# The moving operand of the MLP's matmuls read from the last token to the first

## The chip, the cores and the metric

The kernel runs on one core of a Trainium2 chip. The metric is the time of one execution on the device in microseconds (us). The kernel before takes 845.86 us, the median of three runs (842.13 to 848.72 us).

## The reference

One layer of a hybrid decoder on 512 tokens of 1024 features: an attention branch and a recurrent branch, merged, and then an MLP. The change lies in the MLP alone, which is the last two lines:

```python
h = rmsnorm(x, norm_mix_g[l])
proj = jnp.einsum('bsd,de->bse', h, w_in[l])
...
x = x + jnp.einsum('bsd,de->bse', merged, w_out[l])
h2 = rmsnorm(x, norm_mlp_g[l])
up = jnp.square(jax.nn.relu(jnp.einsum('bsd,df->bsf', h2, w_up[l])))
x = x + jnp.einsum('bsf,fd->bsd', up, w_down[l])
```

Here `h2` is 512 x 1024, `w_up` 1024 x 4096 and `w_down` 4096 x 1024, all float32.

## The kernel before

**Layout.** Features lie on the 128 partitions and tokens along the free axis, so a matmul has a 128 x 128 block of weights as its stationary operand and tokens as its moving operand. The 512 tokens are two halves of 256. TensorE works in float32r; every operand is split into a rounded part (`hi`) and the rest (`lo`), and every product is three matmuls: weights hi by tokens hi, weights hi by tokens lo, weights lo by tokens hi (`for e, (l, r) in enumerate(((hi, 0), (hi, 1), (lo, 0)))`, lines 1387 and 1404). In the profile a weight tile is called `whi` or `wlo`.

**Stages.** The input projection, the attention and the recurrent branch take the first part of the execution, the merge and the output projection follow, and from line 1006 on the kernel does the MLP. Those earlier stages are not touched.

**The MLP by sums of blocks.** The MLP's two matrix products are cut into blocks of two by two: input features by output features by the two halves of tokens. Instead of eight products of blocks, seven are made, each of a sum of weight blocks with a sum of token blocks. They are named M1 to M7 and run in the order of `ORDER7`. The token blocks, and the sums and differences of them, are called forms:

- `h2` holds the eight forms of the MLP's input, `h2[:, r, i, f]`, with r the hi or lo part, i one of four groups of input features, and f the form; one form is 256 tokens of one half, and they lie next to each other in memory (4 bytes a token).
- `us` (the list `forms`) holds the seven forms of the squared activations for one chunk, `forms[n][:, r, f, h]`, again 256 tokens each.

**The work on TensorE.** `steps` lists every product: for four rounds d, the up products of two chunks of hidden features (kinds `up` and `uq`), then the down products (`dn`) of these. The first chunk of all (`pl`, plain) is done without sums: its matmuls take the two halves together, 512 columns. `product_go` issues a product of M1 to M7: 24 matmuls of 256 columns, from four groups of input, two blocks of output and the three hi/lo pairs. `plain_go` issues a plain one. All of them are written to PSUM banks called `acc`.

**After each product.** `up_posts` and `plain_posts` take a bank, add or subtract it elementwise to what the other products gave, apply relu and square and store a quarter; `form_tasks` and `totals` make the next forms from quarters, on ScalarE (ACT) for hi and VectorE (DVE) for lo. `down_posts` adds a bank to `x2`, the residual, which holds 512 tokens in their order, and for the last round scales it by the norm (`r2`) and stores it to `out`. Weights come by DMA from SyncE's queue (SP), some sums of weights by DMAs that accumulate from GpSimd's queue (POOL), and ACT and DVE split them into hi and lo.

**What sets the order.** Each piece of work is a `Task` with an engine and a duration that the program assumes (2.73 us for a product of 24 matmuls; DVE, ACT and load times by formula). A planner lays the tasks out by due times, tries 400 variations with a fixed seed, and issues them in the order of the best one. These durations are constants in the program; the access pattern of a matmul does not enter them.

Of the kernel before, what the change touches and what calls it, by code (L numbers as in the profile page):

```python
# [21 lines left out]
P = 128  # L22
# [17 lines left out]
def tile_block(ctx: ExitStack, tc: tile.TileContext, x, w_in, w_rga, w_rgx, w_pa, w_pr, w_o,  # L40
# [38 lines left out]
    def psum(tag):  # L79
        return pp.tile([P, 512], F32, tag=tag, name=tag, bufs=nb[tag])  # L80
# [230 lines left out]
    with tc.tile_pool(name="p1", bufs=1) as p1:  # L311
# [3 lines left out]
        I = InOrder(nc.tensor)  # L315
# [25 lines left out]
        for k0, k1 in pieces:  # L341
            u, kk = k0 // 4, slice(k0 % 4, (k1 - 1) % 4 + 1)
# [611 lines left out]
    h2 = fin.tile([P, 16 * 1024 + 64], F32R, name="h2")  # L954
    onesr = h2[:, :1]
    h2 = h2[:, 48:48 + 16 * 1024].rearrange("p (r i f s) -> p r i f s", r=2, i=4, f=8)
# [50 lines left out]
    ACT8 = {"M1": 0, "M4": 3, "M2": 2, "M5": 4, "M6": 5, "M7": 6, "M3": 7}  # L1007
# [44 lines left out]
    act = lambda columns: 0.1 + 0.00085 * columns  # L1052
    raw, units, quads, forms, banks = {}, {}, {}, [None] * 8, {}
# [250 lines left out]
    I = InOrder(nc.tensor)  # L1304
# [70 lines left out]
    def product_go(o, pairs, u, fresh):  # L1375
        kind, a, p = o
        b, f = (kind, a, BANK.get(p, "Y")), FORM[p]
        split_y = kind == "dn" and a[0] == 3 and b[2] == "Y"

        def go():  # L1380
            if fresh:
                banks[b] = (*banks.get(b, ()), psum("acc")) if split_y else psum("acc")
            hi, lo = units[o]
            for v in range(u.start, u.stop):
                d = banks[b][v][:, :256] if split_y else banks[b][:, 256 * v:256 * v + 256]
                for z, i in enumerate(pairs):
                    for e, (l, r) in enumerate(((hi, 0), (hi, 1), (lo, 0))):
                        act = h2[:, r, i, ACT8[p]] if kind != "dn" else forms[2 * a[0] + i // 2][:, r, f, i % 2]
                        I.matmul(d, l[:, i, P * v:P * v + P], act, start=fresh and z == e == 0 and (v == 0 or split_y),
                                 stop=i == 3 and e == 2, skip_group_check=True)  # L1390
        return go

    def plain_go(o, half):
        kind, a, p = o
        oc, kc = int(p[1]) % 2, int(p[1]) // 2

        def go():
            hi, lo = units[o]
            if kc == half == 0:
                for u in range(2):  # L1400
                    banks[kind, a, oc, u] = psum("acc")
            for m in range(4 * half, 4 * half + 4):
                u, i = (m // 4, m % 4) if kc else (m % 2, m // 2)
                for e, (l, r) in enumerate(((hi, 0), (hi, 1), (lo, 0))):
                    I.matmul(banks[kind, a, oc, u], l[:, i, P * u:P * u + P], h2[:, r, i, 2 * kc:2 * kc + 2], start=kc == i == e == 0, stop=kc == 1 and i == 3 and e == 2)
        return go

    for kind, a, p, pairs in steps:
        o = kind, a, p
        if kind == "pl":  # L1410
            oc, kc = int(p[1]) % 2, int(p[1]) // 2
# [190 lines left out]
```

## Time and profile before

| | us |
|---|---|
| median of three runs | 845.86 |
| lowest and highest run | 842.13, 848.72 |
| the profiled execution | 841.17 |
| its span, first to last instruction | 839.3 |
| the MLP's first matmul, from the span's start | 524.26 |

The mean granted clock of TensorE in the profiled execution is 0.999 of full speed. DMA moves 126.08 MB, on average 150 GB/s.

How to read the lines of the profile: a page has the busy time of each engine (PE is TensorE's matmuls, PEld its weight loads, DVE VectorE, ACT ScalarE, POOL GpSimd), a chain of work followed back from the last instruction, and groups of instructions. A group's line gives source line, engine, operation, output and input tile, shape and count, then after the bar busy time in us and the mean of one in ns, then the idle time before it and what ended it. L69 is the line of a helper that records the order of instructions; nearly everything in the MLP goes through it, so its groups are told apart by tile. Matmuls are pipelined: the mean duration of one is longer than the distance between two starts. A row of the timeline begins with the start and the duration in us; a row of the windows gives, for a stretch from one time to another, its length and then each engine's busy time and count, the granted clock, the share of DMA and GB/s.

### The profile page before, as it was taken

Reading aid. Unit: us, or ns where it says so; the run is one execution under the profiler, and the core shown is the slowest. Engines: PE = TensorE matmul, PEld = TensorE weight load, DVE = VectorE, ACT = ScalarE, POOL = GpSimd, SP = SyncE. Lnnn points to the kernel's source line nnn. Section 1 sums busy time; section 2 is a strip of 40 time slices with the busy share of each in tenths; the row PEclk is TensorE's granted clock in tenths of the full one; section 3 lists DMA queues with packets and bytes.
Section 4 is the critical chain, followed back from the end, with each engine's and each line's share of the span. In section 5 each row is a group of like instructions: output and inputs, shape, how many; then the busy total and the mean of one; then the engine's idle time right before and its main releaser. Section 6 shows DMA issues by size and latency. Waiting matters only on the chain.

```text
span 839.3 us, 14359 instructions
## 1 busy us (share of the span) xinstructions
PE 831.4 (99%) x5679; PEld 764.0 (91%) x5679; DVE 656.0 (78%) x1077; ACT 478.4 (57%) x753; POOL 104.2 (12%) x132
## 2 busy tenths in 40 slices
PE   9999999999999999999999999999999999999997
PEld 7899999999988888888888888899999999999997
DVE  6776688887877345978766767899889969977997
ACT  7445456565655334595663345784478358645932
POOL 0042231413201101111111000000000000000000
PEclk9999999999999999999999999999999999999999
DMA  5347232333322247656667672355565576566554
GB/s 202 122 151 222 89 107 71 103 115 97 88 79 76 88 138 209 197 171 187 178 199 165 207 258 74 101 151 152 178 174 146 158 256 171 141 166 198 151 160 117
DMA packets 41171, 126.08 MB, mean 150 GB/s; under 512 B 4992, under 2 KB 9800, under 8 KB 41104
## 3 DMA queue, kind: packets, MB, share of 16 engines
q1 hardware_dynamic: 31152, 92.65, 33.6%
q0 software_dynamic: 9952, 32.53, 17.7%
q8 instruction: 44, 0.72, 0.4%
q14 instruction: 23, 0.19, 0.1%
HBM read 102.05 MB, written 11.05 MB: 135 GB/s over the span
## 4 chain that ended last, share of the span: by engine, by line
PE 86%; DVE 8%; DMA 3%; issue 1%; ACT 1%; SPq 0%; ACTq 0%; DVEq 0%
PE acc L69 30%; PE acc L139 15%; PE acc L140 15%; PE acc L141 15%; DVE wlo L69 2%; PE at L595 2%; PE at L139 2%; PE at L141 2%; PE at L140 2%; DMA raw<-in_w_dn_dram 1%; PE at L631 1%; PE at L529 1%; DMA wraw<-in_w_in_dram 1%; DVE raw L69 1%; DVE x L69 1%
## 5 line engine op out<-in xcount | busy, mean ns | idle before, releaser
L69 ACT CAST whi<-raw 128x1024 fp32r<-128x1024 f32 x109 | 111.8, 1049 | 86.8 <-DVE raw L69 26.8
L69 PE MATMUL acc<-us,whi 128*128 128x256 f32 x896 | 153.6, 277 | 0.6 <-ACT us L69 0.4
L69 PE MATMUL acc<-h,whi 128*128 128x256 f32 (+1 forms) x848 | 153.2, 285 | 0.0
L69 DVE TENSOR_TENSOR wlo<-wraw,whi 128x1024 fp32r<-128x1024 f32 (+2 forms) x86 | 96.9, 1148 | 71.7 <-ACT whi L69 65.5
L69 DVE TENSOR_TENSOR wlo<-raw,whi 128x1024 fp32r<-128x1024 f32 x109 | 131.0, 1219 | 21.5 <-ACT whi L69 21.4
L69 PEld LDWEIGHTS acc<-us,whi 128*128 128x128 f32 x896 | 135.1, 188 | 1.1 <-ACT us L69 0.6
L69 PEld LDWEIGHTS acc<-h,whi 128*128 128x128 f32 x848 | 130.1, 188 | 2.6
L69 PE MATMUL acc<-us,wlo 128*128 128x256 f32 x448 | 124.0, 277 | 0.9 <-DVE wlo L69 0.9
L69 PE MATMUL acc<-h,wlo 128*128 128x256 f32 (+1 forms) x424 | 120.6, 285 | 0.0
L69 ACT CAST whi<-wraw 128x1024 fp32r<-128x1024 f32 (+2 forms) x86 | 82.5, 982 | 45.5 <-DMA wraw<-in_w_in_dram 30.4
L139 PE MATMUL acc<-whi,hT 128*128 128x256 f32 x384 | 108.4, 282 | 0.0
L140 PE MATMUL acc<-wlo,hT 128*128 128x256 f32 x384 | 107.2, 279 | 0.2 <-DVE wlo L69 0.2
L69 PEld LDWEIGHTS acc<-us,wlo 128*128 128x128 f32 x448 | 84.3, 188 | 1.1 <-DVE wlo L69 1.1
L139 PE MATMUL acc<-hT,whi 128*128 128x512 f32 x208 | 81.7, 393 | 0.0
L141 PE MATMUL acc<-hT,wlo 128*128 128x512 f32 x208 | 81.1, 390 | 0.0
L69 PEld LDWEIGHTS acc<-h,wlo 128*128 128x128 f32 x424 | 79.6, 188 | 1.3
L141 PE MATMUL acc<-whi,hT 128*128 128x256 f32 x288 | 80.2, 279 | 0.0
L69 ACT ACTIVATE pe<-pe,nm 128x128 f32<-128x128 f32 (+3 forms) x64 | 35.6, 558 | 66.2 <-DVE nm L69 66.2
L140 PEld LDWEIGHTS acc<-wlo,hT 128*128 128x128 f32 x384 | 72.5, 189 | 0.6 <-DVE wlo L69 0.4
L139 PEld LDWEIGHTS acc<-whi,hT 128*128 128x128 f32 x384 | 72.3, 188 | 0.5 <-issue 0.2
L69 POOL TENSOR_TENSOR rs<-ms,mhalf 128x8 f32<-128x8 f32 (+1 forms) x25 | 39.4, 1579 | 187.7 <-DVE ms L69 187.7
L69 POOL DMA_DIRECT2D raw<-raw x24 | 20.7, 864 | 325.0 <-DMA raw<-in_w_up_dram 89.4
(208 smaller groups left out, 1749.3 us busy)
## 6 DMA issues: line engine op xcount, KB each, us to landing
wraw<-in_w_in_dram SPq DMA_DIRECT2D x54, 512.0 KB, 3.6
raw<-in_w_dn_dram SPq DMA_DIRECT2D x32, 512.0 KB, 4.3
raw<-in_w_up_dram SPq DMA_DIRECT2D x29, 512.0 KB, 4.2
raw<-raw POOLq DMA_DIRECT2D x24, 512.0 KB, 4.6
sum<-in_w_up_dram POOLq DMA_DIRECT2D x18, 512.0 KB, 5.5
wraw<-in_w_pa_dram SPq DMA_DIRECT2D x8, 512.0 KB, 4.6
wraw<-in_w_pr_dram SPq DMA_DIRECT2D x8, 512.0 KB, 4.2
wraw<-in_w_o_dram SPq DMA_DIRECT2D x8, 512.0 KB, 5.1
```

What stands on the lines that cost most here:

```text
L69: ins = f(*a, **k)
L139: T.matmul(o, l[0], r[0], start=first, stop=False)
L140: T.matmul(o, l[0], r[1], start=False, stop=False)
L141: T.matmul(o, l[1], r[0], start=False, stop=last)
L529: T.transpose(out=ps[:, t * P:(t + 1) * P], in_=qn[t // 2][:, c0:c0 + P], identity=ident)
L595: T.matmul(lg[c][:, :N], qT[:, c, i * P:(i + 1) * P], qk[h % 2, z][:, c, :N], start=z == 1, stop=z == 2)
L631: T.transpose(out=tp[:, b * P:(b + 1) * P], in_=st[s][:, b * P:(b + 1) * P], identity=ident)
```

## The change

Three operands get a last index of `::-1`. In `product_go` the moving operand of the up products (a form of `h2`) and of the down products (a form of `us`) is read from token 255 of its half down to token 0. In `plain_go` the two halves stay in their order, and each is read backwards.

```diff
-                        act = h2[:, r, i, ACT8[p]] if kind != "dn" else forms[2 * a[0] + i // 2][:, r, f, i % 2]
+                        act = h2[:, r, i, ACT8[p], ::-1] if kind != "dn" else forms[2 * a[0] + i // 2][:, r, f, i % 2, ::-1]
                         I.matmul(d, l[:, i, P * v:P * v + P], act, start=fresh and z == e == 0 and (v == 0 or split_y),
                                  stop=i == 3 and e == 2, skip_group_check=True)
...
-                    I.matmul(banks[kind, a, oc, u], l[:, i, P * u:P * u + P], h2[:, r, i, 2 * kc:2 * kc + 2], start=kc == i == e == 0, stop=kc == 1 and i == 3 and e == 2)
+                    I.matmul(banks[kind, a, oc, u], l[:, i, P * u:P * u + P], h2[:, r, i, 2 * kc:2 * kc + 2, ::-1], start=kc == i == e == 0, stop=kc == 1 and i == 3 and e == 2)
```

A matmul writes its columns in the order in which it reads them, so every bank of the up products holds the tokens of a half in reverse, and so do the quarters and the forms made from it, since all that lies between is elementwise. The down products read those forms backwards once more, which puts the tokens into their old order in the banks that are added to `x2`. The weights, the addresses, the number of matmuls and the two matmuls of the norm (`norm_go`) are as before.

## Prediction

> **What bounds the kernel now.** I read the page's busy shares first, then its chain of work that ended last, then windows over the MLP, then the timeline of TensorE (PE) alone.
>
> ```profile
> span 839.3 us, 14359 instructions
> PE 831.4 (99%) x5679; PEld 764.0 (91%) x5679; DVE 656.0 (78%) x1077; ACT 478.4 (57%) x753; POOL 104.2 (12%) x132
> PEclk9999999999999999999999999999999999999999
> PE 86%; DVE 8%; DMA 3%; issue 1%; ACT 1%; SPq 0%; ACTq 0%; DVEq 0%
> ```
>
> TensorE is busy 99% of the span, the granted clock is in its top tenth in every slice, and 86% of the chain runs over TensorE. A change that alters how long one matmul holds the array therefore goes straight into the time. The next rows are the groups of the MLP (by line, shapes kept apart) and its start in the timeline.
>
> ```profile
> L69 PE MATMUL acc<-us,whi 128*128 128x256 f32 x896 | 153.6, 277 | 0.6 <-ACT us L69 0.4 <-DVE x L69 0.2
> L69 PE MATMUL acc<-h,whi 128*128 128x256 f32 x784 | 133.5, 276 | 0.0
> L69 PE MATMUL acc<-us,wlo 128*128 128x256 f32 x448 | 124.0, 277 | 0.9 <-DVE wlo L69 0.9
> L69 PE MATMUL acc<-h,wlo 128*128 128x256 f32 x392 | 108.2, 276 | 0.0
> L69 PE MATMUL acc<-h,whi 128*128 128x512 f32 x64 | 19.7, 389 | 0.0
> L69 PE MATMUL acc<-h,wlo 128*128 128x512 f32 x32 | 12.5, 389 | 0.0
> 524.26 0.62 PE L69 MATMUL acc<-h,whi 128*128 128x512 f32 x2
> ```
>
> The MLP runs from 524.26 us to the end. It has 896 + 784 + 448 + 392 = 2520 matmuls of 256 columns and 64 + 32 = 96 of 512; these are exactly the ones the change touches. TensorE's waits in these groups add up to 0.6 + 0.9 = 1.5 us, so the stage is bound by the matmuls themselves. The means of 276 and 277 ns are not what one matmul costs: they overlap. The cost is the distance from one start to the next. Stretches without a wait give it:
>
> ```profile
> core 0: us, PE busy (x) PEld busy (x) DVE busy (x) ACT busy (x) POOL busy (x), PEclk, DMA share, GB/s
> 571.60:628.90 57.30, 57.30 (x506) 57.30 (x507) 52.04 (x58) 30.33 (x37) 3.45 (x4) 1.00 0.63 177
> 660.50:792.80 132.30, 132.30 (x1170) 132.30 (x1169) 110.78 (x123) 84.43 (x108) 8.50 (x10) 1.00 0.62 176
> 821.20:834.90 13.70, 13.70 (x117) 13.70 (x118) 11.30 (x19) 2.17 (x3) 0.86 (x1) 1.00 0.41 109
> ```
>
> 132.30 us over 1170 matmuls is 113.1 ns each, and 57.30 over 506 is 113.2 ns. The last stretch is different: 13.70 over 117 is 117.1 ns, at the same granted clock of 1.00. So the same instruction on the same kind of operands has two paces. The timeline of TensorE around a short wait shows the change from one to the other:
>
> ```profile
> 642.59 0.28 PE L69 MATMUL acc<-us,wlo 128*128 128x256 f32 x1
> ...
> 647.69 0.28 PE L69 MATMUL acc<-us,wlo 128*128 128x256 f32 x1
> 648.14 0.47 PE L69 MATMUL acc<-us,whi 128*128 128x256 f32 x2 [0.17 <-DVE x L69]
> 648.45 0.28 PE L69 MATMUL acc<-us,wlo 128*128 128x256 f32 x1
> 648.80 0.28 PE L69 MATMUL acc<-us,wlo 128*128 128x256 f32 x1
> 649.15 0.28 PE L69 MATMUL acc<-us,wlo 128*128 128x256 f32 x1
> 649.51 0.28 PE L69 MATMUL acc<-us,wlo 128*128 128x256 f32 x1
> ```
>
> Products come in triples, so two wlo starts are three matmuls apart. From 642.59 to 647.69 there are 15 triples: 5.10 us / 45 = 113.3 ns. After the wait of 0.17 us, 648.45 to 649.51 are three triples: 1.06 us / 9 = 117.8 ns. The slower pace is therefore a state that a wait can start and that can last; I call the difference, 117.8 - 113.3 = 4.5 ns, the step. It is the only change of pace that the trace shows for these matmuls, and the trace doesn't say what makes it. A weight load runs beside every matmul (PEld is as busy as PE in the windows), so two reads of SBUF, one of the weights and one of the moving tokens, go on at all times; a pace that depends on how these two meet is what I would suspect.
>
> **The change part by part.** Nothing is added, removed or moved: the same 2616 matmuls with the same 2616 weight loads, outputs, waits and order, and no transfer, queue or other engine is touched. The planner's durations for a product are constants, so the order that it writes is the same one. What differs is the direction in which the moving operand is read.
>
> Step 1, the products of 256 columns. They read their half from token 255 down to 0. The cost is 2520 times the change of the pace, whatever that is; all of it lies on the path that sets the end. The trace of before has no operand that is read backwards, so the price is bounded from rows. The lower end is a gain of one step, 4.5 ns (if the backward order met the weight read better): 2520 x 4.5 = -11.3 us. The upper end of an ordinary loss is one step the other way, for those matmuls that do not have it yet. The last stretch has 117 at the slow pace and the one after 648.14 about a dozen: 2520 - 130 = 2390 x 4.5 = +10.8 us. A rougher bound from an earlier stage is the group below, whose mean is 282 ns beside 276 here: 6 ns, or 2520 x 6 = +15.1 us.
>
> ```profile
> L139 PE MATMUL acc<-whi,hT 128*128 128x256 f32 x384 | 108.4, 282 | 0.0
> 524.72 0.39 PE L69 MATMUL acc<-h,wlo 128*128 128x512 f32 x1
> 525.40 0.39 PE L69 MATMUL acc<-h,wlo 128*128 128x512 f32 x1
> 1.19 3.80 PE L69 MATMUL acc<-zero 128*128 128x256 f32 x17 [1.19 <-DVE zero L69]
> ```
>
> The far end is a read that delivers columns at half the rate. Its nearest row is the last one above, the slowest run of 256-column matmuls in the trace: 17 in 3.80 us, 224 ns each (an upper value, as the last one's drain is in it). That is 224 - 113 = 111 ns more, or 2520 x 111 = +279.7 us.
>
> Between these ends I take 0. The reason is a row pair: 512 columns in one matmul cost (525.40 - 524.72) / 3 = 227 ns, twice the 113.3 ns of 256 columns. The price is per column, with no part per instruction that shows, so it is the streaming that is paid for; a backward order asks for the same columns at the same distance of one element from each other. That value is nearest to the forward rows, which are the only ones of these very operands.
>
> [...]
>
> Step 2, the 96 plain products of 512 columns. Their operand becomes two runs of 256, each backwards, where it was one run of 512. Taken as two matmuls of 256 it costs 2 x 113.3 = 226.6 ns beside 227 measured: 96 x 0 = 0 us. One step more per half, 9 ns, would be +0.9 us; one less -0.9; half rate would be 96 x 2 x 111 = +21.3 us.
>
> Step 3, what follows. The banks now hold tokens in reverse within a half. The evacuations, squares, sums and splits are elementwise and see the same shapes: 0 us. The down products read the reversed forms backwards again, so their banks, the final scaling and the stores are as before: 0 us. The cover here is that no instruction of DVE, ACT or a queue changes; if it failed, any of them would be longer and TensorE would wait on DVE, which is busy 52.04 of 57.30 us (91%) in the densest stretch and is what comes late next.
>
> The sum is 0 + 0 + 0. Against the profiled execution's own time of 841.17 us (839.3 us of span and 1.9 us around it) this is 841.2 us. That execution stands 4.7 us below the median of the runs, 845.86 us (842.13 to 848.72). I give the time on the median's scale: **845 us**, rounded.
>
> **The rivals.**
>
> First, the slower one: the slow pace everywhere. Place: all 2616 matmuls. Mechanism: reading from the other end turns round the phase between the moving stream and the weight stream, and the state that now follows a wait becomes the usual one. Price: +10.8 + 0.9 = +11.7 us, or 852.9 us for the profiled execution and 857.6 us on the median's scale. It decides (over 1%, 8.5 us) from 8.5 / 2520 = 3.4 ns per matmul, which is less than the step. For it speaks that the two paces exist for one instruction; against it, that 1170 matmuls in a row over many different tiles hold 113.1 ns, so the fast state is not delicate. [...]
>
> Second, half rate: the array's read cannot stream downwards at full rate. Price: +279.7 + 21.3 = +301 us, 1147 us on the median's scale. For it speaks only that no row shows a backward read; against it, that the step stays one element.
>
> Third, faster: the backward order takes the step away from the usual pace. Price: -11.3 - 0.9 = -12.2 us, 833.7 us on the median's scale, if DVE keeps up; its 91% in the densest stretch would become 52.04 / (57.30 x 108.8 / 113.3) = 95%, so a little of it would come back as waits. [...] Against it: nothing in the trace shows any such matmul below 113 ns.
>
> Fourth, that the change doesn't do what it says: an access pattern could be turned into something else on the way to the chip. The counts would then differ (more matmuls of fewer columns); I hold it to be part of the second rival's chance.
>
> **How the numbers follow.** No change (within 1%) 0.55; slow pace or an ordinary loss of that size 0.17; half rate or another heavy loss 0.16; faster 0.12. About 1% is what a measurement of this kernel can tell from no change. So faster by over 1% is 0.12, within 1% 0.55, slower by over 1% 0.33. The range goes from the third rival, 834 us, up to the rough bound of an ordinary loss: 845.86 + 15.1 + 0.9 = 861.9, and some 3 us more for the runs' own spread (845.86 to 848.72), 865 us. It leaves out the heavy case, 0.16. The likeliest case's own range is 842 to 849 us, that of the runs before.
>
> **What would show each step right or wrong.** Right: start-to-start distances of 113 ns in the long stretches of the MLP and 227 ns for the 96 plain ones, counts of 896, 784, 448, 392, 64 and 32 unchanged, the MLP beginning near 524 us as before. The first rival shows as some 1170 matmuls in 138 us instead of 132.30 with PEclk still at 1.00, the second as a doubled distance and DVE's share falling to about half, the third as 109 ns and new waits of PE on DVE wlo. If the distances are unchanged and the span is not, the prediction is wrong outside its steps, in the waits or the transfers that this change should leave alone.

## The result, and the profile after

| | kernel before | changed kernel |
|---|---|---|
| median of 20 runs, us | 847.41 | 850.79 |
| lowest and highest | 840.68, 852.42 | 849.27, 856.96 |
| profiled execution | 841.17 | 851.39 |
| its span | 839.3 | 849.6 |

The changed kernel takes 1.007 times as long as the one before (95% interval 1.0047 to 1.0094): slower by some 0.7%, within the 1% that the prediction called no change, but clear of zero. The two profiled executions are farther apart, 10.2 us or 1.2%. Why the profiled executions differ by more than the medians is part of the finding.

The page of the changed kernel first: its span, the busy engines and the clock, and the chain of work that ended last.

```profile
span 849.6 us, 14359 instructions
PE 843.2 (99%) x5679; PEld 775.0 (91%) x5679; DVE 656.1 (77%) x1077; ACT 479.9 (56%) x753; POOL 103.7 (12%) x132
PEclk9999999999999999999999999999999999999999
PE 88%; DVE 5%; ACT 3%; DMA 2%; issue 1%; SPq 0%; ACTq 0%; DVEq 0%
```

TensorE's busy time rose by 11.8 us (831.4 to 843.2) with the same count of instructions. DVE and ACT are as busy as before (656.0 and 656.1, 478.4 and 479.9 us) and the granted clock is the same (0.999 and 1.000). So the time went into the matmuls themselves. The windows of the changed kernel, over the same stretches as before, show how:

```profile
571.60:628.90 57.30, 57.30 (x487) 57.14 (x486) 50.47 (x56) 28.01 (x34) 3.00 (x4) 1.00 0.61 175
660.50:792.80 132.30, 132.30 (x1126) 132.30 (x1125) 106.50 (x119) 77.85 (x98) 8.60 (x10) 1.00 0.61 171
```

In the same 132.30 us there are 1126 matmuls where there were 1170. A window also counts a matmul that only overlaps its edge, and a matmul overlaps one or two others (276 ns long at 113 ns from start to start in the kernel before), so the count is about 2.5 too high. Taking that off, 132.30 / 1123.5 = 117.8 ns, where the kernel before has 132.30 / 1167.5 = 113.3 ns. From here on paces are worked out in this way. The plain products changed, too, as the groups and the timeline of the changed kernel show:

```profile
L69 PE MATMUL acc<-h,whi 128*128 128x512 f32 x64 | 20.6, 401 | 0.2 <-DVE h L69 0.2
524.88 0.40 PE L69 MATMUL acc<-h,wlo 128*128 128x512 f32 x1
525.58 0.40 PE L69 MATMUL acc<-h,wlo 128*128 128x512 f32 x1
```

Their mean is 401 ns where it was 389, and the distance is (525.58 - 524.88) / 3 = 233 ns where it was 227. The 0.2 us at the end of the first row is TensorE's only listed wait in the MLP, where the kernel before had 1.5 us.

The sum of the two profiles: 2390 matmuls x 4.5 ns = +10.8 us (the prediction's count of those that had the fast pace), 96 x 6.5 ns = +0.6 us (the means of the distances are 233.3 and 226.8 ns), waits 0.2 - 1.5 = -1.3 us, together +10.1 us. The spans differ by 849.6 - 839.3 = 10.3 us. Nothing of size is left over.

### The profile page after: what moved, and what is told of

It reads as the page before. It is cut to its first block, busy times and chain, and to the rows that moved or that the text cites. A ratio compares the mean times of both kernels' runs of the same rounds, so it can differ in the third digit from the quotient of the medians.

```text
span 849.6 us, 14359 instructions
## 1 busy us (share of the span) xinstructions
PE 843.2 (99%) x5679; PEld 775.0 (91%) x5679; DVE 656.1 (77%) x1077; ACT 479.9 (56%) x753; POOL 103.7 (12%) x132
## 4 chain that ended last, share of the span: by engine, by line
PE 88%; DVE 5%; ACT 3%; DMA 2%; issue 1%; SPq 0%; ACTq 0%; DVEq 0%
PE acc L69 37%; PE acc L139 14%; PE acc L140 14%; PE acc L141 13%; PE at L595 2%; PE at L139 2%; PE at L140 2%; PE at L141 2%; DVE wlo L69 2%; DMA wraw<-in_w_o_dram 1%; PE at L631 1%; ACT whi L69 1%; PE at L529 1%; PE at L668 1%; DMA xT<-in_x_dram 1%
## 5 line engine op out<-in xcount | busy, mean ns | idle before, releaser
L69 PE MATMUL acc<-h,whi 128*128 128x256 f32 (+1 forms) x848 | 159.2, 291 | 0.2 <-DVE h L69 0.2
L69 PE MATMUL acc<-us,whi 128*128 128x256 f32 x896 | 158.7, 282 | 0.0
```

What stands on the lines that cost most here:

```text
L69: ins = f(*a, **k)
```

## The experiments

The theory at the start was that the pace hangs on how the moving read and the weight read meet in SBUF ("phase", later "meeting"). That was the author's guess, from two paces of one instruction (113.3 and 117.8 ns) with a weight load beside every matmul (1169 beside 1170 in 132.30 us); no run here shows such a meeting. By it, moving the weights should undo what turning the read round had done, and of blocks of tokens their order alone should count. Its rival was that a backward read costs by itself ("direction"). In the tables below, a pace is 100 us over the count less 2.5, from the window of 680 to 780 us, in which none of these kernels has a wait of TensorE. A time is one run, unless a range stands with it; the kernel before ran beside it.

### Weights moved by 64 or 128 bytes, in both directions

```diff
-            units[o] = weight_pair((0 if own else 64) if o[0] != "pl" else 192 if own else 0, fin if own else None)
+            units[o] = weight_pair((((0 if own else 64) if o[0] != "pl" else 192 if own else 0) + 64) % 256, fin if own else None)
```

This is put on the changed kernel (`rev_w64`) and on the kernel before (`fwd_w64`); `rev_w128` and `fwd_w128` add 128 in place of 64. The sum is taken modulo 256, so a tile that lay at 192 goes to 0 or 64.

> The changed kernel, with every weight tile of the MLP moved by 64 bytes. [...] Direction theory (a backward read costs 4 ns per 256 columns wherever it starts): 117 ns and about 850 us, as in the changed kernel.

> The kernel before, reading forward, with every weight tile of the MLP moved by 64 bytes. [...] Direction theory: 113.3 ns and about 840 us.

> The changed kernel, with every weight tile of the MLP moved by 128 bytes. Meeting theory with a period of 128 bytes: as the changed kernel, 117.8 ns. With a period of 256 bytes or more: another pace, between 113 and 121 ns. Direction theory: 117.8 ns.

> The kernel before, with every weight tile of the MLP moved by 128 bytes. Meeting theory with a period of 128 bytes: 113.3 ns, as in the kernel before, since 64 bytes gave 118.7 ns and another 64 close the period. With a longer period: another pace, 116 to 121 ns. Direction theory: 113.3 ns.

The window's rows, in the order rev_w64, fwd_w64, rev_w128, fwd_w128:

```profile
680.00:780.00 100.00, 100.00 (x836) 100.00 (x835) 77.89 (x86) 57.69 (x72) 5.16 (x6) 1.00 0.62 180
```
```profile
680.00:780.00 100.00, 100.00 (x845) 100.00 (x845) 78.90 (x87) 57.87 (x73) 5.16 (x6) 1.00 0.62 179
```
```profile
680.00:780.00 100.00, 100.00 (x836) 100.00 (x835) 77.58 (x85) 57.44 (x72) 5.16 (x6) 1.00 0.62 179
```
```profile
680.00:780.00 100.00, 100.00 (x851) 100.00 (x851) 79.14 (x87) 58.43 (x75) 5.16 (x6) 1.00 0.62 182
```

| kernel | pace, ns | time, us | kernel before, us |
|---|---|---|---|
| rev_w64 | 120.0 | 855.87 | 849.15 |
| fwd_w64 | 118.7 | 852.22 | 849.15 |
| rev_w128 | 120.0 | 857.65 | 850.48 |
| fwd_w128 | 117.9 | 851.33 | 850.48 |

The two runs with 64 bytes go against both theories. Moving the weights did not bring the backward read to 113.3 ns, it made it slower (120.0 beside 117.8); and the forward read lost its 113.3 ns without being turned round (118.7). The runs with 128 bytes go against the direction theory and against a period of 128 bytes; they lie in the ranges that a longer period left, but these held nearly every pace there is here. One window of a forward stream is weak evidence, as the repeats of the kernel before will show: 117.9 ns occurs with the weights in their old place, too. The address of the weights still mattered to a forward stream. That is seen at the very start of the MLP, before any wait: the forward plain products had a mean of 389 ns in the kernel before, and have it in all six profiles here that read them forward with whole blocks of weights in their old place (before, before_a, before_b, fwd_kick, fwd_wide, dn_back). They have 395 in fwd_w64, in the row below, and in fwd_w128.

```profile
L69 PE MATMUL acc<-h,whi 128*128 128x512 f32 x64 | 20.1, 395 | 0.0
```

So where the weights lay changed the mean of matmuls whose moving operand had not been touched, from 389 to 395 ns. What makes the difference, the rows don't show.

### Blocks of 16 tokens: only the order of the blocks, or only the order within a block

```diff
+                        act = act.rearrange("p (g c) -> p g c", c=16)[:, ::-1, :]
```

This is `lines_back`, put on the forward operand; `inline_back` has `[:, :, ::-1]` instead. The plain products get the same within each half.

> Each half is read in blocks of 16 tokens (64 bytes): the blocks from last to first, the 16 tokens in a block forward. [...] Direction theory, if what costs is the step of -1 from token to token: 113.3 ns. If blocks cost something by themselves: more than 117 ns.

> Each half is read in blocks of 16 tokens (64 bytes): the blocks from first to last, the 16 tokens in a block backward. [...] Direction theory, if what costs is the step of -1 from token to token: 117 ns.

Rows of the window, lines_back and then inline_back:

```profile
680.00:780.00 100.00, 100.00 (x851) 100.00 (x850) 78.47 (x88) 58.52 (x74) 5.64 (x7) 1.00 0.61 179
```
```profile
680.00:780.00 100.00, 100.00 (x752) 100.00 (x752) 74.98 (x82) 53.05 (x66) 6.88 (x8) 1.00 0.53 141
```

lines_back ran at 100 / 848.5 = 117.9 ns (850.72 us), the changed kernel's pace, and from its first products to the end, although its tokens go forward within every 64 bytes. So a step of -1 from token to token is not needed for that pace; turning round the order of the blocks is enough. This is one profile, without disturbances, and a forward stream can be at 117.8 ns as well. But the single distances, which the section on one kind of product explains, are those of a backward stream here. The reverse mixture was a surprise: inline_back ran at 100 / 749.5 = 133.4 ns (891.91 us), slower than anything else here and than either theory had it (113.3 ns by the phase theory, 117 by the direction theory). Why a jump after every 16 tokens added nothing to the changed kernel's pace in one kernel (117.9 ns) and 15.5 ns in the other (133.4) is open.

### Weights read from one column

```diff
-                        I.matmul(d, l[:, i, P * v:P * v + P], act, start=fresh and z == e == 0 and (v == 0 or split_y),
+                        I.matmul(d, l[:, i, P * v:P * v + 1].broadcast_to([P, P]), act, start=fresh and z == e == 0 and (v == 0 or split_y),
```

The matmul of `plain_go` gets the same. This is put on the kernel before (`fwd_onecol`) and on the changed kernel (`rev_onecol`). If the pace hangs on how the two reads meet, both directions should then have one pace.

> [...] Direction theory: 113.3 ns here.

> The changed kernel (backward), with every weight load of the MLP reading one column 128 times, as in the run before it. Meeting theory: the same pace as in that run, within 0.5 ns. Direction theory: some 4 ns slower than that run (117 to 118 ns).

Rows of the window, fwd_onecol and then rev_onecol; behind each a row of the same kernel from the first up products (TensorE alone: length, busy time and count, clock, DMA):

```profile
680.00:780.00 100.00, 100.00 (x860) 100.00 (x859) 79.58 (x88) 61.20 (x78) 6.03 (x7) 1.00 0.61 177
```
```profile
551.00:565.00 14.00, 14.00 (x126) 1.00 0.57 175
```
```profile
680.00:780.00 100.00, 100.00 (x852) 100.00 (x851) 78.49 (x88) 59.52 (x76) 6.03 (x7) 1.00 0.59 176
```
```profile
551.00:565.00 14.00, 14.00 (x121) 1.00 0.54 157
```

Forward it ran at 116.6 ns and backward at 117.7 ns (847.95 and 849.98 us), so the meeting theory fell: with the weight read standing still, the directions should have been alike within 0.5 ns. But the plain direction theory doesn't hold either, as 116.6 is not 113.3. The second row gave the next idea. In 551 to 565 us, its first up products, the same forward kernel ran at 14.00 / 123.5 = 113.4 ns, where the backward one has 14.00 / 118.5 = 118.1; it has 116.6 ns only after the one listed wait of TensorE in its MLP (0.4 us, on ACT). One kernel, one direction, two steady paces. So a new theory: the pace is a pattern that the stream of matmuls falls into when it starts or is interrupted, and then keeps.

### The kernel before, twice more

> The kernel before, unchanged, once more. Its runs lie in two groups, about 841 to 843 and 846 to 852 us. Locked-pace theory (the pace of the matmuls is a steady pattern that is set when the stream starts or is interrupted, and forward reading has both a 113.3 ns pattern and slower ones): a run of the upper group shows the MLP's matmuls at 116 to 120 ns for most of the MLP, with no more waits than before. Other theory (the groups come from waits on transfers): 113.3 ns in both groups and 5 to 9 us more of waits in the upper one.

> As the run before it: a second draw of the kernel before, with the same two expectations.

Two stretches of before_a, and the same two of before_b:

```profile
575.00:630.00 55.00, 55.00 (x469) 55.00 (x469) 48.20 (x53) 28.91 (x36) 3.44 (x4) 1.00 0.57 167
670.00:720.00 50.00, 50.00 (x443) 50.00 (x442) 41.17 (x46) 32.85 (x44) 2.84 (x4) 1.00 0.69 196
```
```profile
575.00:630.00 55.00, 55.00 (x488) 55.00 (x487) 49.71 (x55) 30.95 (x39) 3.44 (x4) 1.00 0.60 168
670.00:720.00 50.00, 50.00 (x427) 50.00 (x426) 39.81 (x44) 33.19 (x44) 2.58 (x3) 1.00 0.66 194
```

before_a (842.68 us) ran 55.00 / 466.5 = 117.9 ns in the first stretch and 50.00 / 440.5 = 113.5 in the second; before_b (845.81 us) the other way round, 113.3 and then 117.8. It is the same program, at the same clock. The forward stream has two patterns, and a short wait can move it from one to the other: before 648.14 us the kernel before has 113 or 114 ns from start to start, and behind the wait of 0.17 us there 117 to 119. It need not: all three profiles of this kernel have the same wait of 0.4 us on ACT near 570 us, and only before_a runs at 117.8 ns behind it. Nor need the wait be long: before_b changes between 647 and 649 us, where TensorE has no listed wait, only two places where the starts fall behind by some 0.15 and 0.26 us. From the MLP's first matmul to its last, the profiled executions of 841.17, 842.68 and 845.81 us take 311.0, 312.6 and 316.3 us, so nearly all that sets them apart lies in the MLP. The runs of the kernel before are spread over 840.68 to 852.42 us, eight of twenty below 844 and the others above 845. That the slowest of them have 117.8 ns nearly throughout fits this, but none of the runs above 846 us is profiled here, so it is not shown. The execution that the prediction worked from was one of the former, with nearly all its MLP at 113.3 ns. The changed kernel has no run below 849.27.

### Some forty short disturbances, forward and backward

```diff
+                        if fresh and z == e == 0 and v == u.start:
+                            n = 16 * (1 + 5 * len(kicks) % 16)
+                            kicks.append(n)
+                            I.matmul(d[:, :n], l[:, i, P * v:P * v + P], act[:, :n], start=True, stop=False, skip_group_check=True)
```

Here `kicks` is a list that starts empty. What the extra matmul writes is written over by the next one.

> The kernel before, with a short extra matmul ahead of the first one into each fresh bank of the MLP (16 to 256 columns, another width each time; what it writes is written over), which shifts the stream's phase about a hundred times. Locked-pace theory: the pace changes from product to product, and some of them run at 113.3 ns, others at 116 to 120 ns. Direction theory: 113.3 ns throughout, whatever the shift.

> The changed kernel with the same extra matmuls. If the backward read has the 113.3 ns pattern too and merely started in a slower one: some products at 113.3 ns, about as many as in the forward run. If the backward read doesn't have that pattern: no product below about 116.5 ns, though the pace changes from product to product.

Four stretches between disturbances of fwd_kick, then three of rev_kick (length, TensorE's busy time and count, clock, DMA):

```profile
571.50:585.50 14.00, 14.00 (x126) 1.00 0.62 179
588.90:594.20 5.30, 5.30 (x47) 1.00 0.39 74
595.20:608.20 13.00, 13.00 (x117) 1.00 0.59 213
608.60:613.80 5.20, 5.20 (x47) 1.00 0.84 293
```
```profile
572.40:587.40 15.00, 15.00 (x130) 1.00 0.63 176
597.00:607.50 10.50, 10.50 (x92) 1.00 0.57 201
637.20:648.00 10.80, 10.80 (x92) 1.00 0.62 177
```

Forward: 113.4, 119, 113.5, 117 ns; the stream goes to and fro between two paces, 113.3 and 117.8 (the short stretches are rough). Backward: 117.6, 117.3, 120.7 ns. Over the whole of rev_kick the stretches lie at 117.5 to 118.1 or at 120.0 ns; none is near 113.3. This is the run that decides: a backward stream was disturbed 47 times (not the hundred that the expectation named), by widths from 16 to 256 columns, and never fell into the 113.3 ns pattern that the forward one reached again and again. The times are 851.97 and 858.08 us, beside 843.71 for the kernel before.

### One kind of product backward

```diff
+                        act = act[:, ::-1] if kind == "dn" else act
```

This is `dn_back`, on the forward operand; `up_back` is the changed kernel without the `::-1` on the down products.

> Only the down products (1344 matmuls) read backward; the forms they read are not reversed, so the two halves of what the MLP adds come out with their tokens reversed. If the direction of a matmul alone sets its pace: 117.8 ns in the down products, 113.3 ns in the up products after them. If a pattern, once slow, is carried on by the matmuls that follow: 117.8 ns in the up products from the second round on as well, until a wait happens to set the fast pattern.

> Only the plain and up products (96 and 1176 matmuls) read backward, and the result's tokens are reversed within each half for the MLP's part. If the direction alone sets the pace: about 117.8 ns in the up products, 113.3 ns in the down products. If the pattern is carried on: the down products, reading forward, stay at 117.8 ns until a wait happens to set the fast pattern.

Stretches of dn_back: backward down products of the first round, forward up products of the second, forward up products of the third. Below them up_back: forward down products of the first round with backward up products of the second, then forward down products of the second, then backward up products of the third.

```profile
572.00:605.50 33.50, 33.50 (x287) 1.00 0.53 158
606.00:640.00 34.00, 34.00 (x303) 1.00 0.66 200
690.00:724.00 34.00, 34.00 (x291) 1.00 0.55 143
```
```profile
575.00:645.00 70.00, 70.00 (x597) 1.00 0.60 173
656.00:685.00 29.00, 29.00 (x258) 1.00 0.67 200
686.00:725.00 39.00, 39.00 (x333) 1.00 0.62 175
```

dn_back: 117.8, 113.1 and 117.9 ns. up_back: 117.7, 113.5 and 118.0 ns. The backward products are at 117.8 in every row. The forward ones can be at either: dn_back's were back at 113.3 ns in the second round and at 117.8 in the third, and up_back's at 117.7 in the first round and 113.5 in the second.

It looks as if the slow pattern were carried on into forward products sometimes. The single distances say otherwise. The trace holds starts to the nanosecond, and products come in triples. In a backward stretch of these two kernels, the three distances of a triple are 115, 118 and 120 ns (now and then 119 for 118), over and over. In a forward stretch at 117.8 ns, here and in before_a and before_b, they are 117 to 119 ns. Both add up to some 353 ns a triple, so the two have one mean and are still two patterns. In a forward stretch at 113.3 ns they are 113 or 114 ns.

At each of the fourteen places where these two kernels go over from one kind of product to the other, the distances change to those of the new direction within four matmuls, and there is no wait at any of them. Where forward turned to backward it was always 115, 118 and 120; where backward turned to forward it was 113.3 ns five times and 117 to 119 ns twice (dn_back at 684 us, up_back at 568 us). So in these two kernels the direction of the read set the pattern within four matmuls, and the backward pattern is not carried on. What chooses between the two forward ones is open. lines_back has the 115, 118 and 120 of a backward read throughout. The changed kernel has distances from 114 to 121 ns, with the same mean. rev_onecol is the exception: with the weights read from one column, its backward read has 117 to 119.

The times, 847.87 and 847.64 us, are single runs inside the range of the kernel before beside them (13 runs, 840.36 to 850.81 us), so they don't say what each half of the change costs.

### Putting the forward stream right on purpose

```diff
+                        if fresh and z == e == 0 and v == u.start and p == "M1":
+                            I.matmul(banks[b][v] if split_y else banks[b], l[:, i, P * v:P * v + P], h2[:, 0, 0, 0:2], start=True, stop=False, skip_group_check=True)
```

> The kernel before with one extra matmul of 512 columns ahead of the first product of every group of seven (some 15 of them, about 3.6 us; what they write is written over). [...] If that restores the fast pattern: every group starts at 113.3 ns, whatever the one before it ran at, a span of about 843 us and runs that lie closer together than those of the kernel before, which could be some 1 to 3 us below it in the median. If not: groups at 117.8 ns after a wait as before, and some 3 us more than the kernel before.

Four groups of seven products in a row, each begun by a wide matmul:

```profile
587.70:606.20 18.50, 18.50 (x165) 1.00 0.50 147
606.70:626.10 19.40, 19.40 (x167) 1.00 0.71 215
626.60:645.20 18.60, 18.60 (x167) 1.00 0.60 165
645.70:665.50 19.80, 19.80 (x169) 1.00 0.47 141
```

113.8, 117.9, 113.1, 118.9 ns: the wide matmul doesn't restore the pattern, it changes over from one to the other each time (with some 165 matmuls to a stretch these are rough by up to 1 ns; the single starts give 113.3 and 117.8 in turn). The expectation failed, and the kernel is slower than the one before: 851.22 us (849.1 to 853.16), ratio 1.0056 (1.0021 to 1.0091). No version here was shown to be faster than the kernel before.

## Why the prediction was wrong

**What bounds the kernel: right.** The MLP hangs on the distance between matmuls; all of the difference was found there.

**Step 1 failed.** It took a backward read of 256 columns for free, because the price looked like one per column and the distance from token to token stayed one element. The pair of rows behind this, 227 ns for 512 columns and 113.3 for 256, compares two forward streams, and cannot tell what a backward one costs. The change measured 4.5 ns on each of 2390 matmuls, +10.8 us between the profiles, the upper end of an ordinary loss that the step itself had named. What it lacked: the 113.3 ns were not the price of a column but one of two patterns of the forward stream, and the backward stream was never seen in it (rev_kick, and the fourteen changes of direction in dn_back and up_back). That the loss came out as one step, 4.5 ns, is luck: the step was read from the forward stream's own slow pattern, and the backward stream has another one with the same mean.

**Step 2** was 0 and measured 6.5 ns on 96 matmuls, +0.6 us. The comparison with two matmuls of 256 was nearly sound, but with those at 117.8 ns, not at 113.3: twice 117.8 is 235.6, and 233.3 was measured.

**Step 3: right.** DVE and ACT kept their busy time, and TensorE's waits fell from 1.5 to 0.2 us, likely because slower matmuls gave DVE more time (busy 50.47 of 57.30 us where it was 52.04; an estimate of the author's).

**The scale failed, too.** The prediction said that its execution stood 4.7 us below the median and moved its sum onto the median as it was. (0 on that scale is 845.86, which rounds to 846 and not to 845.) That gap was the finding in small: runs of the kernel before already have part of the MLP at 117.8 ns (before_a, before_b), so the change can take less from its median than from the profiled execution. 10.2 us between the profiles became 3.4 us between the medians.

**The first rival** had the pace right: 1126 matmuls in 132.30 us at clock 1.00, where it named 1170 in 138, and 852.9 us for the profiled execution where 851.39 was measured. Its time on the median's scale, 857.6, was too high for the reason just given. The argument held against it, that 1170 matmuls in a row at 113.1 ns show the pattern not to be delicate, was wrong: before_b loses it in the middle of the MLP, between 647 and 649 us, and has 117.8 ns in 670 to 720 us and in 740 to 790. The rival's mechanism is another matter. The state that follows a wait did not become the usual one, since the backward read has its own pattern (115, 118 and 120 ns); and the phase between the two reads is not shown: with the weight read on one column, the directions still differ (116.6 and 117.7 ns).

**The others fell.** Half rate: the cost is 4% (4.5 of 113.3 ns), not 100%. Faster: no 24 backward matmuls in a row are below 117.7 ns in the changed kernel, and no stretch of rev_kick is near 113.3. The change left out on the way to the chip: counts are unchanged and the pace is not.

The measured 850.79 us lies in the range, and within 1%, but the forecast was 845 and no change, and there was one. That the number is so near is luck: the loss that step 1 put at nothing shows in the median as a third of its size, because the kernel before is slow in many of its own runs.

## What to carry to other kernels

Before pricing a change to a stage that is bound by matmuls, look at the distance between starts over the whole stage, not at one mean: two steady values at one granted clock (here 113.3 and 117.8 ns at 1.00) show that the stream has patterns, and a change can cost the difference without touching any work (here 4.5 ns on each of 2390 matmuls). When the profiled execution does not stand at the median of its runs, ask what the others did before moving a sum from one to the other; two more profiles of the same kernel would have shown it. Keep the moving operand forward and contiguous where there is a choice: no other order tried here was seen at 113.3 ns (the windows of 100 us have 117.7 to 133.4). And a mean can hide a difference: two streams of 117.8 ns were told apart only by their single distances.

## What the runs showed that was not expected

The paces of 256-column matmuls are a handful of steady values, not a spread: 113.3, 116.6, 117.8, 118.7, 120.0 and 133.4 ns in these kernels, all at clock 1.00. A short extra matmul (fwd_kick) or a wait of 0.17 us (the kernel before, at 648 us) moved the stream from one to another; it then stayed there for more than a hundred matmuls in two of the stretches of fwd_kick above, for eleven behind that wait, and to the end of the MLP, some 117, behind one of 0.9 us at 820 us. A change of direction did so within four matmuls, without a wait (dn_back, up_back). Moving the weights by 64 bytes altered which values came up, in one profile for each direction (118.7 forward, 120.0 backward). What in the chip makes these patterns, and why a backward order of 64-byte blocks was never seen in the lowest one, stays open; so does the 133.4 ns of blocks that go forward with their tokens going backward.
